# RWKV-7 time mixing on one core: transpositions, masks and head sums moved within a head pair's chain

## The chip, the cores and the metric

The program runs on 1 core of one Trainium2 chip. Its engines are TensorE (PE; PEld is its weight load), VectorE (DVE), ScalarE (ACT), GpSimd (POOL) and SyncE, whose queue (SP) issues nearly all DMAs here. The metric is the device time of one execution in microseconds (us); lower is better. Three runs of the kernel before the change gave 2665.36, 2665.69 and 2669.86 us, so the median is 2665.69 us.

## The reference, cut to what matters

The whole model is two layers: time mixing (RWKV-7) and a squared-ReLU MLP, then banded attention and an MLP, on 256 tokens of width 2048. Only time mixing is touched. It has 32 heads of 64 channels.

```python
def rwkv7_time_mix(h, mu, w_r, w_k, w_v, w_o, w0, w1, w2, a0, a1, a2, g1, g2, k_k, k_a, r_k, ln_w, ln_b):
    xr, xw, xk, xv, xa, xg = [h + xx * mu[j] for j in range(6)]
    r, k, v = xr @ w_r, xk @ w_k, xv @ w_v
    w_log = -jax.nn.softplus(-(w0 + jnp.tanh(xw @ w1) @ w2)) - 0.5
    a = jax.nn.sigmoid(a0 + (xa @ a1) @ a2)
    g = jax.nn.sigmoid(xg @ g1) @ g2
    kk = heads(k * k_k)
    kk = kk / jnp.maximum(jnp.sqrt(jnp.sum(kk * kk, axis=-1, keepdims=True)), 1e-12)
    k = k * (1 + (a - 1) * k_a)
    decay = jnp.exp(-jnp.exp(heads(w_log)))
    def step(S, inp):
        r_t, w_t, k_t, v_t, kk_t, a_t = inp
        sa = jnp.einsum('bhvk,bhk->bhv', S, -kk_t)
        S = (S * w_t[:, :, None, :] + sa[..., None] * (kk_t * a_t)[:, :, None, :]
             + v_t[..., None] * k_t[:, :, None, :])
        return S, jnp.einsum('bhvk,bhk->bhv', S, r_t)
    ...  # y from the scan, normalized per head, plus sum(r k r_k) v, times g, through w_o
```

## The kernel before, in words

The recurrence is computed in chunks of 64 tokens (C = 64, four chunks) for two heads at a time; the class `Pair` is one such pair, and there are 16 of them. Channels lie on the 128 partitions (two heads of 64), tokens on the free axis. A pair is a generator of 36 steps (each `yield` ends one): `early`, 8 steps, makes the decays (`sw`, `cum`, `e1`, `e2`), the normalized key `kk` (from the head sum `pss` of `sq`, a matmul with the block matrix `bones`), and the products `bh`, `kh`, `kr`, `rkp`, `vp`; `invert`, 12 steps, makes the inverse of a unit triangular 64x64 matrix per head and chunk; `late`, 16 steps, walks the four chunks with the state `zs`, and then normalizes `y`, with a second head sum `var`.

`invert` starts from the Gram product `gr` (tile `pg`, line 210). ACT copies its blocks out as `da` and `co` (lines 218 and 220); `u` starts as identity plus a masked `da` (line 221 on POOL, line 227 on DVE), and `als` (line 223, POOL) holds the masked blocks of four more levels. Each level l of the loop at line 237 takes two steps: first a transposition of `u` on DVE (line 239, tile `tt`), 32x32 matmuls of it with `als` into the PSUM tile `iv`, and a copy `xs` by ACT; then matmuls of `xs` with `u` and an update of `u` on DVE (line 254). In the last level `uf` is written: its diagonal blocks by POOL (line 249), its corner by DVE (line 258).

The order of the work is set by the loop over slots in `layer_a` (line 889). A pair starts every 8 slots, so up to five pairs are alive, at steps 8 apart. In each slot every living pair takes one step, pairs in `invert` first, then `late`, then `early`; the PE work of each is put behind that of the one before by `issue_after`. Behind these small matmuls PE gets a piece of dense work: four of the 32 k-tile pieces of this pair of heads' k and r projections (line 853; lines 412 and 413 are their matmuls), or, when all projections are done, of the output projection. In three slots of four, from slot 16 on, one piece of an adaLN vector is accumulated on DVE (line 454, tile `acc`, from a 512 KB load of `w_ada`, tile `raw`). Weights come in fp32 and are split into two halves: `wH` by an ACT cast (line 378), `wL` by a DVE subtraction (line 381).

```python
for _, _, pr in sorted(live, key=lambda x: x[:2]):
    with tc.issue_after(last):
        next(pr.gen)
    last = self.last_pe()
```

PE's order is so written out; each of the other engines takes its queue in order too, and the framework's planner fills that queue: what comes earlier in the program goes first when it is expected to be ready. Waits between engines, and waits for a buffer of a tile to come free, are set by the framework, which also keeps two engines from accessing one PSUM bank tile at once in an order other than the program's. PSUM tiles: `gr` and `iv` have one buffer, `ms` (all products of odd kinds, through `psm`) two, `lt` (a bank of `late`) two, `pj` (projections) two. SBUF tiles `s`, `sl`, `bh`, `kh`, `u`, `tt`, `xs` and the like rotate over the number of buffers given at the call.

Of the kernel before, what the change touches and what calls it, by code (L numbers as in the profile page):

```python
# [25 lines left out]
C = 64  # L26
# [51 lines left out]
class Pair:  # L78
# [43 lines left out]
    def early(self):  # L122
# [19 lines left out]
        pss = b.psm()[:, :T]  # L142
        self.head_sums(pss, sq)
# [8 lines left out]
        yield  # L152
        rs, ss, rr = s(), s(), s()
# [16 lines left out]
        nc.vector.tensor_tensor(out=kr[:, :, 0:C], in0=ch(kk), in1=e0, op=ALU.mult)  # L170
        nc.vector.tensor_tensor(out=self.bh, in0=self.bh, in1=kk, op=ALU.mult)
        nc.vector.tensor_tensor(out=kr[:, :, C:P], in0=ch(r), in1=e1, op=ALU.mult)
        rkp = s()
        nc.vector.scalar_tensor_tensor(out=rkp, in0=r, scalar=vec("r_k", j), in1=km, op0=ALU.mult, op1=ALU.mult)
# [17 lines left out]
    def invert(self):  # L192
# [11 lines left out]
        ts = []  # L204
        for src in (bh, kh):
            t = s()
            nc.gpsimd.tensor_tensor(out=ch(t), in0=ch(src), in1=self.pc.to_broadcast([P, 4, C]), op=ALU.mult)
# [4 lines left out]
        nc.vector.tensor_tensor(out=ch(ar), in0=pg[:, :, C:P], in1=ui[:, :, C:P], op=ALU.mult)  # L212


        da, co, u = half("da", 2), half("co", 2), half("u", 2)
        for i, K in enumerate(QS):
            n = H * (i % 2)
            nc.scalar.copy(da[K], pg[K, :, n:n + H])
# [1013 lines left out]
```

## Time and profile before

| | before |
|---|---|
| median of three runs | 2665.69 us |
| the profiled execution's own time | 2668.82 us |
| span of the profiled execution | 2667.0 us |
| PE busy | 2594.2 us, 97% |
| DVE busy | 2112.8 us, 79% |
| ACT busy | 1345.2 us, 50% |
| POOL busy | 208.7 us, 8% |
| mean granted TensorE clock | 0.992 |

The time mixing's pairs run from about 219 to 715 us of the span. A row of a group reads: line, engine, operation, output<-inputs, shapes, count, then busy time in us, mean ns of one, and the idle time of the engine just before them with what ended it. A row of a timeline reads: start in us, duration in us, engine, line, operation, operands, count, and in brackets the idle time before it and what ended that. Consecutive instructions of one kind are merged in a timeline. A row of a table by stretch reads: stretch, length, busy us and count of PE, PEld, DVE, ACT, POOL, then the granted clock as a share of full speed, the busy share of the DMA engines and GB/s. PE's ends are modelled, so a busy PE may hide short waits.

### The profile page before, as it was taken

To read this page: it belongs to the slowest core of one execution; us is meant where nothing else is said; L and a number is where in the kernel's file an instruction comes from. 1 tells how busy PE (TensorE), PEld (TensorE's weight loads), DVE (VectorE), ACT (ScalarE), POOL (GpSimd) and SP (SyncE) were. 2 spreads that over 40 slices of the span, in tenths; PEclk is the share of its full clock that TensorE was granted. 3 is DMA by queue.
4 is the path that set the end of the run, shared out by engine and by line. 5 is a ranking of instruction groups with operands and counts; after the bars stand their busy time and mean duration, and the time that the engine had idled before them with its cause. 6 is when DMAs were issued, how large, how long until landed. Compare 5 with 4: busy or idle time off the path is not lost.

```text
span 2667.0 us, 58173 instructions
## 1 busy us (share of the span) xinstructions
PE 2594.2 (97%) x23596; PEld 2229.2 (84%) x23596; DVE 2112.8 (79%) x3102; ACT 1345.2 (50%) x2435; POOL 208.7 (8%) x320
## 2 busy tenths in 40 slices
PE   7999999999999999999999999999999999999997
PEld 4787777887899888888888998877898888888886
DVE  6788888889789888888888898899887555555555
ACT  3346455555456445355365554565564463453554
POOL 0002223322110000000001100000100000000002
PEclk9999999999999999999999999999999999999998
DMA  9976556566778888889898679887766555555553
GB/s 349 312 244 211 185 179 207 180 214 199 246 236 312 309 317 327 319 324 332 318 329 293 238 242 331 318 274 256 265 218 235 190 189 184 188 189 186 186 189 119
DMA packets 207149, 662.62 MB, mean 248 GB/s; under 512 B 21408, under 2 KB 54560, under 8 KB 206880
## 3 DMA queue, kind: packets, MB, share of 16 engines
q1 hardware_dynamic: 204816, 656.36, 71.5%
q8 instruction: 185, 3.03, 0.5%
q10 hardware_dynamic: 2064, 2.54, 0.3%
q14 instruction: 84, 0.69, 0.1%
HBM read 656.72 MB, written 2.10 MB: 247 GB/s over the span
## 4 chain that ended last, share of the span: by engine, by line
PE 85%; DVE 5%; issue 4%; DMA 4%; ACT 2%; POOL 1%; DVEq 0%; SPq 0%; ACTq 0%; POOLq 0%
PE pj L412 45%; PE pj L413 23%; PE pj L402 2%; PE pj L401 2%; PE pj L403 2%; DMA raw<-w_ada 1%; DVE wL L381 1%; PE iv L111 1%; DVE acc L454 1%; PE gr L105 1%; ACT wH L378 1%; PE ms L115 1%; PE o L401 1%; PE ms L324 0%; PE ms L105 0%
## 5 line engine op out<-in xcount | busy, mean ns | idle before, releaser
L381 DVE TENSOR_TENSOR wL<-raw,wH 128x1024 fp32r<-128x1024 f32 x772 | 941.1, 1220 | 354.9 <-ACT wH L378 347.0
L378 ACT CAST wH<-raw 128x1024 fp32r<-128x1024 f32 x772 | 805.8, 1045 | 799.7 <-PE pj L412 650.0
L412 PE MATMUL pj<-aHL,wH 128*128 128x512 f32 x3328 | 1202.0, 403 | 1.9 <-DVE x L945 1.4
L413 PE MATMUL pj<-aHL,wL 128*128 128x256 f32 x3328 | 936.1, 281 | 0.4 <-DVE wL L381 0.4
L412 PEld LDWEIGHTS pj<-aHL,wH 128*128 128x128 f32 x3328 | 629.4, 189 | 154.4 <-issue 8.7
L412 PE MATMUL pj<-hHL,wH 128*128 128x512 f32 x2048 | 723.0, 398 | 0.0
L413 PEld LDWEIGHTS pj<-aHL,wL 128*128 128x128 f32 x3328 | 629.4, 189 | 3.1 <-issue 0.8
L413 PE MATMUL pj<-hHL,wL 128*128 128x256 f32 x2048 | 574.4, 281 | 0.0
L412 PEld LDWEIGHTS pj<-hHL,wH 128*128 128x128 f32 x2048 | 384.6, 188 | 94.4 <-DVE hHL L991 0.2
L413 PEld LDWEIGHTS pj<-hHL,wL 128*128 128x128 f32 x2048 | 386.8, 189 | 0.1
L454 DVE SCALAR_TENSOR_TENSOR acc<-rada,ct,acc 128x1024 f32<-128x1024 f32 x256 | 327.2, 1278 | 8.5 <-DMA rada<-w_ada 7.6
L518 POOL TENSOR_TENSOR ss<-ss,sq 128x256 f32<-128x256 f32 x56 | 52.6, 940 | 1590.8 <-ACT sq L517 1590.5
L1016 DVE SCALAR_TENSOR_TENSOR x<-pj,mod,x 128x256 f32<-128x256 f32 x256 | 123.4, 482 | 58.6 <-PE pj L413 54.9
L454 DVE SCALAR_TENSOR_TENSOR acc<-raw,ct,acc 128x1024 f32<-128x1024 f32 x104 | 136.2, 1309 | 15.3 <-DMA raw<-w_ada 14.9
L988 ACT ACTIVATE t<-t 128x256 f32<-128x256 f32 x112 | 46.8, 418 | 123.5 <-DVE t L960 123.5
L401 PE MATMUL pj<-aHL,wH 128*128 128x258 f32 x384 | 109.0, 284 | 0.0
L402 PE MATMUL pj<-aHL,wH 128*128 128x258 f32 x384 | 108.9, 284 | 0.0
L403 PE MATMUL pj<-aHL,wL 128*128 128x258 f32 x384 | 108.0, 281 | 0.0
L403 PEld LDWEIGHTS pj<-aHL,wL 128*128 128x128 f32 x384 | 73.2, 191 | 0.2
L402 PEld LDWEIGHTS pj<-aHL,wH 128*128 128x128 f32 x384 | 72.6, 189 | 0.1
L401 PEld LDWEIGHTS pj<-aHL,wH 128*128 128x128 f32 x384 | 72.2, 188 | 0.2
L990 ACT ACTIVATE t<-t 128x256 f32<-128x256 f32 x128 | 53.4, 417 | 3.4
(249 smaller groups left out, 2815.5 us busy)
## 6 DMA issues: line engine op xcount, KB each, us to landing
raw<-w_up SPq DMA_DIRECT2D x256, 512.0 KB, 4.2
raw<-w_down SPq DMA_DIRECT2D x256, 512.0 KB, 4.3
rada<-w_ada SPq DMA_DIRECT2D x209, 512.0 KB, 5.8
raw<-w_ada SPq DMA_DIRECT2D x111, 512.0 KB, 4.3
rada<-w_ada_kv SPq DMA_DIRECT2D x64, 512.0 KB, 6.1
rawa<-w_ada SPq DMA_DIRECT2D x32, 512.0 KB, 6.9
rawa<-w_ada_t SPq DMA_DIRECT2D x32, 512.0 KB, 7.5
raw<-w_k SPq DMA_DIRECT2D x32, 512.0 KB, 4.0
```

The costliest lines, as they stand in the source:

```text
L378: nc.scalar.copy(Hf, raw)
L381: eng.tensor_tensor(out=Lf, in0=raw, in1=Hf, op=ALU.subtract)
L401: nc.tensor.matmul(ps, H[:, i, :], a(kt)[:, 0, :], start=(first and kt == 0), stop=False)
L402: nc.tensor.matmul(ps, H[:, i, :], a(kt)[:, 1, :], start=False, stop=False)
L403: ins = nc.tensor.matmul(ps, L[:, i, :], a(kt)[:, 0, :], start=False, stop=(last and kt == KT - 1))
L412: nc.tensor.matmul(ps, H[:, i, :], a(kt), start=(kt == 0), stop=False)
L413: ins = nc.tensor.matmul(ps[:, 0, :], L[:, i, :], a(kt)[:, 0, :], start=False, stop=(kt == KT - 1))
L454: nc.vector.scalar_tensor_tensor(out=self.acc, in0=raw, scalar=ck, in1=self.acc, op0=ALU.mult, op1=ALU.add)
L518: (eng or nc.gpsimd).tensor_tensor(out=self.ss, in0=self.ss, in1=sq, op=ALU.add)
L988: nc.scalar.activation(t, t, AF.Relu)
L990: nc.scalar.activation(t, t, AF.Square)
L1016: nc.vector.scalar_tensor_tensor(out=x, in0=ps[:, i, :], scalar=self.mods[(layer, 5)][:, n:n + 1], in1=x, op0=ALU.mult, op1=ALU.add)
```

## The change

Nothing is computed differently but for the order of some operations and the engine that does them.

- In `invert`, the transposition of `u` is no longer the first instruction of a level but the last of the update before it: a helper `turned()` issues it directly behind the start value of `u` (in the first step) and directly behind each update.
- The identity is added to `u` by GpSimd, directly behind the mask, ahead of `als`; it was DVE's, one step later.
- `ar` (the masked right half of `pg`) moves from the first step, ahead of the copies `da` and `co`, to the second.
- The corner of `uf` is copied by ACT instead of DVE.
- The factors scaled by `pc` (`ts`, two GpSimd multiplications) move from the first step of `invert` to the seventh of `early`, two steps ahead.
- In `early`, the head sum `pss` goes from the third step to the fifth; `ss` and the three activations behind it from the fourth to the fifth; `rr`, `rs` and `kk` from the fifth to the sixth; `bh`'s second product and `kr` from the sixth to the seventh. `vp` comes earlier, from the seventh to the fifth, and `rkp` from the sixth to the fifth; `km` and `kh` stay in their steps.
- In `late`, the square of `y` is taken in the last chunk's step, the head sum `var` two steps behind it, in the free half of the pair's own bank instead of an `ms` tile, and the logarithm and the addition of `v` one step earlier.

```diff
@@ -139,8 +139,6 @@
         nc.scalar.activation(sw, sw, AF.Exp, scale=-1.0, bias=b.col(C_MHALF))
         nc.scalar.activation(a, a, AF.Exp, scale=-1.0)
         yield
-        pss = b.psm()[:, :T]
-        self.head_sums(pss, sq)
         cum = s()
         nc.vector.tensor_tensor_scan(out=cum, data0=cst("reset"), data1=sw, initial=0.0, op0=ALU.mult, op1=ALU.add)
         e0, e1 = e01[:, :, 0:C], e01[:, :, 1:C + 1]
@@ -150,35 +148,41 @@
         self.pc = pw.tile([P, 4, 1], F32, tag="pc", bufs=4, name="pc")
         nc.gpsimd.tensor_copy(self.pc, e01[:, :, C:C + 1])
         yield
+        km = s()
+        nc.gpsimd.tensor_scalar(out=km, in0=a, scalar1=-1.0, scalar2=vec("k_a", j), op0=ALU.add, op1=ALU.mult)
+        self.bh, self.kh = s("bh", 2), s("kh", 2)
+        nc.gpsimd.tensor_tensor(out=self.bh, in0=a, in1=e2, op=ALU.mult)
+        yield
+        pss = b.psm()[:, :T]
+        self.head_sums(pss, sq)
         rs, ss, rr = s(), s(), s()
         nc.vector.tensor_scalar(out=ss, in0=pss, scalar1=1e-24, scalar2=None, op0=ALU.max)
         nc.scalar.activation(rs, ss, AF.Ln)
         nc.scalar.activation(rs, rs, AF.Exp, scale=-0.5)
         nc.scalar.activation(rr, rs, AF.Square)
-        km = s()
-        nc.gpsimd.tensor_scalar(out=km, in0=a, scalar1=-1.0, scalar2=vec("k_a", j), op0=ALU.add, op1=ALU.mult)
-        self.bh, self.kh = s("bh", 2), s("kh", 2)
-        nc.gpsimd.tensor_tensor(out=self.bh, in0=a, in1=e2, op=ALU.mult)
-        yield
+        self.vp = pw.tile([P, 4, C], F32, tag="vp", bufs=4, name="vp")
+        pt = b.psm().rearrange("p (a c k) -> p a c k", a=2, c=4)
+        self.each(lambda c: pt[:, 0, c, :], lambda c: ch(v)[:, c, :], lambda c: cst("cen"))
+        nc.scalar.copy(self.vp, pt[:, 0])
+        nc.vector.scalar_tensor_tensor(out=km, in0=km, scalar=1.0, in1=k, op0=ALU.add, op1=ALU.mult)
+        rkp = s()
+        nc.vector.scalar_tensor_tensor(out=rkp, in0=r, scalar=vec("r_k", j), in1=km, op0=ALU.mult, op1=ALU.mult)
+        yield
+        kr = self.kr = self.big("kr", 4)
         nc.vector.scalar_tensor_tensor(out=rr, in0=rr, scalar=-0.5, in1=ss, op0=ALU.mult, op1=ALU.mult)
         nc.vector.scalar_tensor_tensor(out=rs, in0=rr, scalar=1.5, in1=rs, op0=ALU.add, op1=ALU.mult)
         kk = s()
         nc.vector.scalar_tensor_tensor(out=kk, in0=k, scalar=vec("k_k", j), in1=rs, op0=ALU.mult, op1=ALU.mult)
-        nc.vector.scalar_tensor_tensor(out=km, in0=km, scalar=1.0, in1=k, op0=ALU.add, op1=ALU.mult)
-        yield
-        kr = self.kr = self.big("kr", 4)
+        nc.vector.tensor_tensor(out=self.kh, in0=km, in1=e2, op=ALU.mult)
+        yield
+        nc.vector.tensor_tensor(out=self.bh, in0=self.bh, in1=kk, op=ALU.mult)
         nc.vector.tensor_tensor(out=kr[:, :, 0:C], in0=ch(kk), in1=e0, op=ALU.mult)
-        nc.vector.tensor_tensor(out=self.bh, in0=self.bh, in1=kk, op=ALU.mult)
         nc.vector.tensor_tensor(out=kr[:, :, C:P], in0=ch(r), in1=e1, op=ALU.mult)
-        rkp = s()
-        nc.vector.scalar_tensor_tensor(out=rkp, in0=r, scalar=vec("r_k", j), in1=km, op0=ALU.mult, op1=ALU.mult)
-        nc.vector.tensor_tensor(out=self.kh, in0=km, in1=e2, op=ALU.mult)
-        yield
-
-        self.vp = pw.tile([P, 4, C], F32, tag="vp", bufs=4, name="vp")
-        pt = b.psm().rearrange("p (a c k) -> p a c k", a=2, c=4)
-        self.each(lambda c: pt[:, 0, c, :], lambda c: ch(v)[:, c, :], lambda c: cst("cen"))
-        nc.scalar.copy(self.vp, pt[:, 0])
+        self.ts = []
+        for src in (self.kh, self.bh):
+            t = s()
+            nc.gpsimd.tensor_tensor(out=ch(t), in0=ch(src), in1=self.pc.to_broadcast([P, 4, C]), op=ALU.mult)
+            self.ts.insert(0, t)
         yield
         pbn = b.psm()[:, :T]
         self.head_sums(pbn, rkp)
@@ -201,33 +205,34 @@
 
 
         ui = cst("ui").unsqueeze(1).to_broadcast([P, 4, P])
-        ts = []
-        for src in (bh, kh):
-            t = s()
-            nc.gpsimd.tensor_tensor(out=ch(t), in0=ch(src), in1=self.pc.to_broadcast([P, 4, C]), op=ALU.mult)
-            ts.append(t)
         pg = pp.tile([P, 4, P], F32, tag="gr", bufs=1, name="gr")
         self.each(lambda c: pg[:, c, :], lambda c: ch(bh)[:, c, :], lambda c: kr[:, c, :])
-        ar = self.ar = s("ar", 3)
-        nc.vector.tensor_tensor(out=ch(ar), in0=pg[:, :, C:P], in1=ui[:, :, C:P], op=ALU.mult)
 
 
         da, co, u = half("da", 2), half("co", 2), half("u", 2)
+
+        def turned():
+            t = half("tt", 2)
+            nc.vector.transpose(out=t.rearrange("p c t -> p (c t)"), in_=u.rearrange("p c t -> p (c t)"))
+            return t
+
         for i, K in enumerate(QS):
             n = H * (i % 2)
             nc.scalar.copy(da[K], pg[K, :, n:n + H])
             if i % 2 == 0:
                 nc.scalar.mul(co[K], pg[K, :, H:C], -1.0)
         nc.gpsimd.tensor_tensor(out=u, in0=da, in1=every("lev0"), op=ALU.mult)
+        nc.gpsimd.tensor_tensor(out=u, in0=u, in1=every("eye_h"), op=ALU.add)
+        tn = turned()
         als = b.pw.tile([P, 4, 4, H], F32, tag="al", bufs=2, name="al")
         nc.gpsimd.tensor_tensor(out=als, in0=da.unsqueeze(1).to_broadcast([P, 4, 4, H]),
                                 in1=cst("levs").rearrange("p (l k) -> p l k", l=4).unsqueeze(2).to_broadcast([P, 4, 4, H]),
                                 op=ALU.mult)
         yield
-        nc.vector.tensor_tensor(out=u, in0=u, in1=every("eye_h"), op=ALU.add)
-
+        ar = self.ar = s("ar", 3)
+        nc.vector.tensor_tensor(out=ch(ar), in0=pg[:, :, C:P], in1=ui[:, :, C:P], op=ALU.mult)
         pt = b.psm().rearrange("p (a c k) -> p a c k", a=2, c=4)
-        for i, t in enumerate(ts):
+        for i, t in enumerate(self.ts):
             self.each(lambda c: pt[:, i, c, :], lambda c: ch(t)[:, c, :], lambda c: cst("eye"))
         bk = self.bk = b.pw.tile([P, 2, 4, C], F32, tag="bk", bufs=3, name="bk")
         nc.scalar.copy(bk, pt)
@@ -235,8 +240,7 @@
         uf = self.u = b.uf[self.j % 2]
         down, up = ((0, 1), (2, 3)), ((1, 0), (3, 2))
         for l in range(1, 6):
-            tt_, xs = half("tt", 2), half("xs", 2)
-            nc.vector.transpose(out=tt_.rearrange("p c t -> p (c t)"), in_=u.rearrange("p c t -> p (c t)"))
+            tt_, xs = tn, half("xs", 2)
             pi = self.corner(l)
             if l < 5:
                 self.tiles(pi, als[:, l - 1], tt_, [(i, i) for i in range(4)])
@@ -252,10 +256,11 @@
             if l < 5:
                 self.tiles(pi, xs, u, [(i, i) for i in range(4)])
                 nc.vector.tensor_tensor(out=u, in0=u, in1=pi, op=ALU.add)
+                tn = turned()
             else:
                 self.tiles(pi, xs, u, up)
                 for K in QS[::2]:
-                    nc.vector.tensor_copy(uf[K, :, H:C], pi[K])
+                    nc.scalar.copy(uf[K, :, H:C], pi[K])
             if l == 2:
                 pg = pp.tile([P, 4, P], F32, tag="gr", bufs=1, name="gr")
                 self.each(lambda c: pg[:, c, :], lambda c: ch(kh)[:, c, :], lambda c: kr[:, c, :])
@@ -307,22 +312,23 @@
                     nc.vector.scalar_tensor_tensor(out=zn, in0=zs, scalar=pc[:, c, :], in1=pch[:, 2, :],
                                                    op0=ALU.mult, op1=ALU.add)
                 zs = zn
+            if c == 3:
+                sq = self.square(py)
             yield
 
-        sq = self.square(py)
-        yield
-        var = b.psm()[:, :T]
+        yield
+        var = bank[:, 0, :]
         self.head_sums(var, sq)
-        yield
         rg = s("sl", 1)
         nc.scalar.activation(rg, var, AF.Ln, scale=1.0 / C, bias=b.col(C_GN))
+        yield
         nc.scalar.activation(rg, rg, AF.Exp, scale=-0.5)
         nc.vector.scalar_tensor_tensor(out=rg, in0=py, scalar=b.vec("ln_w", j), in1=rg, op0=ALU.mult, op1=ALU.mult)
+        nc.vector.scalar_tensor_tensor(out=rg, in0=v, scalar=b.vec("ln_b", j), in1=rg, op0=ALU.add, op1=ALU.add)
         yield
         pg = b.psm()[:, :T]
         for i in range(2):
             mm(pg, lg[:, i, :], self.tg[:, i, :], start=(i == 0), stop=(i == 1))
-        nc.vector.scalar_tensor_tensor(out=rg, in0=v, scalar=b.vec("ln_b", j), in1=rg, op0=ALU.add, op1=ALU.add)
         nc.vector.tensor_tensor(out=v, in0=pg, in1=rg, op=ALU.mult)
         yield
```

More of the change, by code (lines that the diff above doesn't have):

```diff
@@ L166, in early @@
         nc.vector.scalar_tensor_tensor(out=kk, in0=k, scalar=vec("k_k", j), in1=rs, op0=ALU.mult, op1=ALU.mult)
-        nc.vector.scalar_tensor_tensor(out=km, in0=km, scalar=1.0, in1=k, op0=ALU.add, op1=ALU.mult)
-        yield
-        kr = self.kr = self.big("kr", 4)
-        nc.vector.tensor_tensor(out=kr[:, :, 0:C], in0=ch(kk), in1=e0, op=ALU.mult)
-        nc.vector.tensor_tensor(out=self.bh, in0=self.bh, in1=kk, op=ALU.mult)
-        nc.vector.tensor_tensor(out=kr[:, :, C:P], in0=ch(r), in1=e1, op=ALU.mult)
-        rkp = s()
-        nc.vector.scalar_tensor_tensor(out=rkp, in0=r, scalar=vec("r_k", j), in1=km, op0=ALU.mult, op1=ALU.mult)
         nc.vector.tensor_tensor(out=self.kh, in0=km, in1=e2, op=ALU.mult)
         yield
-        self.vp = pw.tile([P, 4, C], F32, tag="vp", bufs=4, name="vp")
-        pt = b.psm().rearrange("p (a c k) -> p a c k", a=2, c=4)
-        self.each(lambda c: pt[:, 0, c, :], lambda c: ch(v)[:, c, :], lambda c: cst("cen"))
-        nc.scalar.copy(self.vp, pt[:, 0])
+        nc.vector.tensor_tensor(out=self.bh, in0=self.bh, in1=kk, op=ALU.mult)
+        nc.vector.tensor_tensor(out=kr[:, :, 0:C], in0=ch(kk), in1=e0, op=ALU.mult)
+        nc.vector.tensor_tensor(out=kr[:, :, C:P], in0=ch(r), in1=e1, op=ALU.mult)
+        self.ts = []
[3 more added lines that the diff above has]
+            self.ts.insert(0, t)
         yield
```

## The prediction

> **What bounds the kernel now.** I read the page's first part, then the table by stretch for the stage that the change touches, then PE's waits there, then the timelines around the longest of them.
>
> ```profile
> span 2667.0 us, 58173 instructions
> 216.00:300.00 84.00, 74.13 (x1180) 60.59 (x1178) 70.06 (x119) 43.37 (x109) 24.44 (x32) 0.94 0.62 200
> 300.00:630.00 330.00, 323.60 (x6786) 265.44 (x6785) 287.28 (x545) 176.69 (x500) 90.56 (x123) 1.00 0.60 192
> 630.00:720.00 90.00, 82.05 (x1575) 71.28 (x1574) 73.06 (x126) 40.30 (x109) 13.72 (x21) 0.99 0.71 236
> ```
>
> The stage of the pairs is 216 to 720. PE is busy 74.1 of the first 84 us, 323.6 of the middle 330, 82.1 of the last 90: it is the bound, and all its idle time is 9.9 + 6.4 + 8.0 = 24.3 us. The change neither adds nor removes a matmul, so the idle time, and time at a lower clock, is all that it can win. DVE is busy 83%, 87% and 81% of the three stretches: it is no bound in the middle but close to one, and its queue is what PE waits for:
>
> ```profile
> PE o L403 <- DVE wL L381: 3.2, 1, 3.2
> PE iv L111 <- DVE tt L239: 12.2, 10, 4.1
> L115 PE MATMUL ms<-s,csts 128*128 128x256 f32 x32 | 11.2, 431 | 1.6 <-DVE s L174 1.6
> L324 PE MATMUL ms<-tg,lg 128*128 128x256 f32 x64 | 17.9, 401 | 2.8 <-issue 1.4 <-DVE s L154 1.2
> ```
>
> Half of PE's idle time is ten waits for the transposition `tt` (12.2 us, the longest 4.1). By stretch they are 8.5, 2.1 and 1.8 us:
>
> ```profile
>   PE iv L111: 8.5, 5
> ...
>   PE iv L111: 2.1, 4
> ...
>   PE iv L111: 1.8, 2
> ```
>
> The two longest show their making. In the first fence `u` was done at 274.39, but its transposition ran at 277.80, behind 3.4 us of other DVE work that the program puts ahead of it; PE had waited since 274.1. In the second, the transposition stood behind an `acc` that waited for its load.
>
> ```profile
> 274.11 0.28 DVE L254 TENSOR_TENSOR u<-u,iv 128x128 f32<-128x128 f32 x1
> ...
> 277.80 0.30 DVE L239 STREAM_TRANSPOSE tt<-u 128x128 f32<-128x128 f32 x1
> ...
> 278.24 0.65 PE L111 MATMUL iv<-tt,al 32*32 32x32 f32 x32 [4.15 <-DVE tt L239]
> ```
>
> ```profile
> 237.10 1.28 DVE L454 SCALAR_TENSOR_TENSOR acc<-raw,ct,acc 128x1024 f32<-128x1024 f32 x1 [0.29 <-DMA raw<-w_ada]
> 238.30 0.30 DVE L239 STREAM_TRANSPOSE tt<-u 128x128 f32<-128x128 f32 x1
> ...
> 238.75 0.45 PE L111 MATMUL iv<-tt,al 32*32 32x32 f32 x32 [2.36 <-DVE tt L239]
> ```
>
> Behind both, the granted clock falls:
>
> ```profile
> 240.00:244.00 4.00, 4.00 (x45) 3.16 (x44) 2.77 (x6) 1.54 (x4) 1.63 (x3) 0.57 0.77 202
> 276.00:288.00 12.00, 9.76 (x168) 8.22 (x170) 7.45 (x12) 2.04 (x5) 1.87 (x2) 0.72 0.48 155
> ```
>
> The lost work is about 4.00 x (1 - 0.57) = 1.7 us and, over the 9.76 busy us of the second, about 9.76 x 0.28 = 2.7 us (taking the stretch's mean clock for its busy part): 4.4 us.
>
> **The change part by part.** *Transposition behind the update.* 80 transpositions stay 80, at 0.30 us. Directly behind `u`, the one of 274.11 would end near 274.7, and PE would start at 274.8 by the same 0.14 us from end to start (278.10 to 278.24), so about 0.7 of the 4.1 us stays; the other waits of the first stretch go wholly as far as `u` itself is in time. The gain there lies between 0 (the wait only moves, see below) and 8.5 - 0.7 + 4.4 = 12.2 us. The `tt` tiles are held a step longer, with two buffers; as both pairs in `invert` write in the same odd slot and their matmuls read in the next, I count nothing for that. What is queued behind the earlier transposition on DVE (`mk`, `zs`, `wL`) comes 0.30 us later, and an `acc` no longer stands ahead of it.
>
> Why not all 12.2: DVE is busy 70.1 of the 84 us. It sheds three or so of the 1.18 us identity additions and two pairs' corner copies (below), near 4.5 us, and so needs at least 65.5; PE without low clock needs 74.1 - 4.4 = 69.7. Both would have to run with almost no idle time for the whole gain. I take 7.5 us, somewhat over half, since the two long waits, which carry the clock with them, are cut by order alone. In the middle and the end the waits are 2.1 + 1.8 = 3.9 us: I take 2.8.
>
> *Identity on GpSimd, corner on ACT, `ar` later.*
>
> ```profile
> L227 DVE TENSOR_TENSOR u<-u,csts 128x128 f32<-128x128 f32 x16 | 18.6, 1161 | 6.3 <-POOL u L221 5.3
> L254 DVE TENSOR_TENSOR u<-u,iv 128x128 f32<-128x128 f32 x64 | 18.1, 282 | 9.0 <-PE iv L111 8.0
> L258 DVE COPY uf<-ms 32x128 f32<-32x128 f32 x32 | 9.0, 281 | 0.9 <-PE ms L111 0.6
> L221 POOL TENSOR_TENSOR u<-da,csts 128x128 f32<-128x128 f32 x16 | 10.8, 672 | 181.2 <-ACT da L218 181.2
> ```
>
> DVE loses 18.6 + 9.0 = 27.6 us; GpSimd gets 16 x 0.67 = 10.8 us (by L221, the same size) and ACT 32 x 0.25 = 8 us (by the 0.25 us copy of the same size in the next fence, at 489.55). Neither is near full (129 and 260 us of the 504 above), so none of this is on PE's path by itself. The identity addition is dear on DVE: 1161 ns against 282 for an update of the same size. What stands beside it is `als` on GpSimd (next fence: 491.72 for 1.09 us, against 491.79 for 1.18). I read this as the two shutting each other out; the transposition, of one input, does not (492.89, two in 0.49 us, beside `uf` copies).
>
> The start of each pair's inverse now reads: `gr`, six ACT copies, mask, identity, transposition. One pair in the middle:
>
> ```profile
> 486.30 1.09 PE L105 MATMUL gr<-kr,bh 64*64 64x128 f32 x16
> ...
> 489.10 0.41 DVE L212 TENSOR_TENSOR ar<-gr,csts 128x256 f32<-128x256 f32 x1
> 489.43 0.87 DVE L132 TENSOR_SCALAR s<-ms,vecs 128x256 f32<-128x256 f32 x2
> 490.21 1.27 DVE L454 SCALAR_TENSOR_TENSOR acc<-raw,ct,acc 128x1024 f32<-128x1024 f32 x1
> 491.41 0.28 DVE L254 TENSOR_TENSOR u<-u,iv 128x128 f32<-128x128 f32 x1
> 491.79 1.18 DVE L227 TENSOR_TENSOR u<-u,csts 128x128 f32<-128x128 f32 x1
> 492.89 0.49 DVE L239 STREAM_TRANSPOSE tt<-u 128x128 f32<-128x128 f32 x2
> ...
> 489.55 0.25 ACT L218 COPY da<-gr 32x128 f32<-32x128 f32 x1 [1.77 <-DVE ar L212]
> ...
> 491.03 0.73 POOL L221 TENSOR_TENSOR u<-da,csts 128x128 f32<-128x128 f32 x1 [11.73 <-ACT da L218]
> 491.72 1.09 POOL L223 TENSOR_TENSOR al<-da,csts 128x512 f32<-128x512 f32 x1
> ...
> 494.35 0.34 PE L111 MATMUL ms<-tt,co 32*32 32x32 f32 x10
> ```
>
> Before, the copies waited 1.77 us for `ar`; with `ar` behind them they can start when ACT is free. From their start to the mask is 491.03 - 489.55 = 1.5 us, then 0.73 + 0.73 + 0.30. If they start near 487.8 (`gr` ends at 487.4), the first transposition ends near 491.1. DVE, in order, may stand before it from 489.1, where it did `ar`: up to 1.7 us idle. Then come the 0.87 and 1.27 us (491.1 to 493.2), the other pair's update (to 493.5) and its transposition (to 493.8). PE took that one at 494.35. So the new wait fits, with 0.5 us to spare, and the planner may fill it with other work. I take 0.13 us for each of 16 pairs, 2 us, between 0 and 16 x 1.3 = 21.
>
> *Scaled factors.* `ts` is as many instructions, and GpSimd already ran ahead to them and waited for `bh`; `bk` needs them in the second step of `invert`, two slots after their new place. Nothing.
>
> ```profile
> POOL s L207 <- DVE bh L171: 103.2, 16, 9.0
> ```
>
> *Head sums.* The 1.6 us wait for `rkp` (L174) should go with `rkp` a step earlier and its sum where it was. With `pss` out of the slots between `var` and the gate's product, and `var` out of the `ms` tiles (eight a pair instead of nine), L324's 1.2 us waits for `ss` (L154) go too. I count 1.4 of the 2.8, as the saturated DVE of the first stretch may delay what follows. Cost: `pss` and `kk` are nearer to `gr`, which needs `bh` and `kr` one slot after they are made instead of two. A slot is 57.2 / 16 = 3.58 us (the two `gr` below lie two pairs apart); DVE ran 1.7 us behind PE in the fence above (487.4 to 489.1). I take nothing; at worst DVE's 1.27 us `acc` stands ahead of `kr` in half the pairs, 8 x 1.27 = 10 us, and at best it is nothing, since no instruction is saved.
>
> ```profile
> 391.06 1.02 PE gr L105 x16
> ...
> 448.29 1.02 PE gr L105 x16
> ```
>
> No DMA is added or passed on SP's queue; `raw` loads start earlier only as their tiles come free earlier, and the DMA engines are busy 0.60 to 0.71. The 3.2 us wait for `wL` at the end stays.
>
> Sum: -7.5 - 2.8 + 2.0 - 1.4 = -9.7 us. The profiled execution would go from 2668.8 to 2659.1; it was 3.1 us above the median, so the median goes from 2665.7 to **2656.0 us**; its own range is 2647 (12.2 + 3.9 + 2.8 us of gains and no cost) to 2660.4.
>
> **Two rules.** The Trainium skill, "SBUF — State Buffer", section "SBUF: two separate sides", says that DVE with two SBUF inputs and a GpSimd instruction that reads SBUF exclude each other for a whole instruction, whoever starts second waiting. The trace agrees (1161 against 282 ns), and it speaks against the change: the identity on GpSimd may wait out an `acc` of 1.28 us. By that rule at its worst the sum would be -9.7 + 16 x 1.28 = +10.8 us; by the row that I took, it is -9.7.
>
> The page "TensorE: Matmul & The Clock Gate", section "What's actually happening", in the Trainium skill, gives about 3.4 us of idle time before the clock halves. By that, a wait of 2.36 us would cost no clock, the clock's part would be 2.7 instead of 4.4 us, and the sum about 1 us smaller; here the clock was 0.57 behind just that wait, so the row decides.
>
> **The rivals.** *The wait moves (no change).* In the first stretch DVE stays the partner bound, and `acc` still stands in its queue when a load is late:
>
> ```profile
> DVE acc L454 <- DMA raw<-w_ada: 14.9, 13, 2.8
> ```
>
> PE then waits for `u` or `wL` where it waited for `tt`. For it: DVE 70 of 84 us. Against it: 3.4 us of the longest wait were order alone. The first stretch's 7.5 becomes 1.5: 2666 - 3.7 = 2662. The planner leaving `tt` behind other work, so that the change doesn't do what it says, ends there too.
>
> *DVE stands before the first transposition (slower).* Place: step one of each `invert`. GpSimd's copies show what waiting beside DVE does: four in 1.59 us once, and in 2.68 where they began beside DVE's identity addition (491.79 to 492.97).
>
> ```profile
> 293.17 1.59 POOL L249 COPY uf<-u 32x128 f32<-32x128 f32 x4 [0.41 <-DVE u L254]
> ...
> 492.76 2.68 POOL L249 COPY uf<-u 32x128 f32<-32x128 f32 x4
> ```
>
> Point of decision: the transposition more than 0.5 us later than 491.1, that is mask and identity at 2.0 us together instead of 1.5. At 1.3 us over it, all pairs lose 16 x 1.3 = 21 us against the 11.7 of the gains: +9.3, 2675. Against it: DVE stands idle then, so no `acc` runs beside GpSimd.
>
> **How the numbers follow.** A measurement of this kernel can tell about 0.2%, 5.3 us, from no change. Forecast 0.60, the wait moves 0.20, slower 0.20: so faster 0.60, same 0.20, slower 0.20. The range 2645 to 2673 takes in the forecast and the second case and leaves out the far end of the slower one and gains beyond 20.7 us; its low end is 2 us below the forecast's own range, for short waits that a busy PE hides.
>
> **What would show it.** Right: L239's share of PE's waits near zero, the clock near 1.00 from 236 to 288, no L227 on DVE, `als` directly behind an addition on GpSimd. Wrong: DVE waiting for GpSimd before L239's successor in 16 places, or PE idle for `u`, `wL` or `gr` in the first stretch as long as before. A loss in the middle stretch, where only 6.4 us were idle, would overturn the argument.

## The result, and the profile after

The change makes the kernel slower: 2676.03 us (median of 7 runs, 2672.48 to 2680.85) against 2667.27 us (7 runs, 2665.36 to 2669.86) for the kernel before beside it. The ratio is 1.0031, with a 95% interval of 1.0019 to 1.0043, so +8.8 us where the forecast was -9.7. The profiled execution took 2676.03 us. First its page: the span, and the busy time of PE.

```profile
span 2674.2 us, 58153 instructions
...
PE 2597.7 (97%) x23596; PEld 2227.9 (83%) x23596; DVE 2091.8 (78%) x3054; ACT 1355.2 (51%) x2467; POOL 212.9 (8%) x336
```

The table by stretch, as in the prediction (stretch, its length, busy time of PE, PEld, DVE, ACT and POOL, granted clock, DMA share, GB/s):

```profile
216.00:300.00 84.00, 76.56 (x1354) 61.83 (x1352) 68.38 (x119) 47.09 (x118) 26.26 (x36) 0.98 0.64 209
300.00:630.00 330.00, 316.99 (x6490) 256.14 (x6478) 265.22 (x493) 178.88 (x509) 87.12 (x132) 1.00 0.59 188
630.00:720.00 90.00, 86.15 (x1692) 74.24 (x1687) 72.82 (x124) 39.99 (x117) 17.84 (x24) 1.00 0.67 221
```

PE is busier than before in the first 84 us (76.6 against 74.1, at a clock of 0.98 against 0.94) and less in the middle 330 (317.0 against 323.6). So the gain came where it was forecast, and the loss is in the middle, where the prediction said that a loss would overturn it. How much, is seen best by the same work in both: the `gr` matmuls of the 4th and the 16th pair, with 12 pairs between them. The view of the tile `gr` in two short windows gives the first and last start in each, before and then after:

```profile
L105 PE MATMUL gr<-kr,bh x16: 269/269/320, 314.6 to 315.4; 64*64 64x128 f32 x16
...
L105 PE MATMUL gr<-kr,bh x16: 269/269/320, 653.6 to 654.5; 64*64 64x128 f32 x16
```

```profile
L105 PE MATMUL gr<-kr,bh x16: 269/269/320, 309.3 to 310.1; 64*64 64x128 f32 x16
...
L105 PE MATMUL gr<-kr,bh x16: 269/269/320, 660.8 to 661.6; 64*64 64x128 f32 x16
```

The 4th pair comes 5.3 us earlier than before (309.3, 314.6), the 16th 7.2 us later (660.8, 653.6): the twelve pairs take 351.5 us instead of 339.0, and lose 12.5. The span grew by the same 7.2 us, so behind the pairs nothing changes. The table by stretch, for just these twelve pairs, splits the loss, before and then after:

```profile
314.60:653.60 339.00, 330.57 (x6946) 271.74 (x6942) 296.75 (x563) 184.34 (x525) 96.83 (x132) 1.00 0.60 194
```

```profile
309.30:660.80 351.50, 336.57 (x6950) 272.74 (x6944) 284.71 (x530) 191.78 (x549) 97.62 (x144) 1.00 0.59 191
```

PE was idle 8.4 us before and 14.9 after (+6.5), and its busy time grew by 6.0 for the same work. DVE did 12.0 us less and yet held PE up. The waits of the stage of the pairs (216 to 725; microseconds in total, times, longest) name a new first for DVE:

```profile
DVE tt L216 <- POOL u L225: 22.3, 16, 1.7
DVE wL L387 <- ACT wH L384: 20.5, 16, 2.4
...
PE iv L111 <- DVE tt L216: 13.5, 16, 2.5
```

DVE stands before the first transposition of all 16 pairs, for the identity on GpSimd: the sign of being wrong that the prediction named. PE's waits for `tt` are no fewer than before (15.7 us, 13.5 at `iv` and 2.2 at `ms`, against 12.2); in the middle 330 us they grew from 2.1 to 9.1, the 7.7 and 1.4 of these rows:

```profile
PE iv L111 <- DVE tt L216: 7.7, 10, 1.4
PE lt L285 <- DVE zs L312: 2.8, 3, 1.2
PE ms L111 <- DVE tt L216: 1.4, 3, 0.6
```

The timeline of one pair's start shows why DVE stands (rows of GpSimd, DVE and PE; start, duration, and in brackets the idle time before):

```profile
490.27 0.73 POOL L224 TENSOR_TENSOR u<-da,csts 128x128 f32<-128x128 f32 x1 [7.82 <-ACT da L221]
...
490.97 2.18 POOL L228 TENSOR_TENSOR al<-da,csts 128x512 f32<-128x512 f32 x1
490.99 1.22 DVE L387 TENSOR_TENSOR wL<-raw,wH 128x1024 fp32r<-128x1024 f32 x1
...
493.12 0.41 POOL L225 TENSOR_TENSOR u<-u,csts 128x128 f32<-128x128 f32 x1
...
493.56 0.31 DVE L216 STREAM_TRANSPOSE tt<-u 128x128 f32<-128x128 f32 x1 [0.96 <-POOL u L225]
```

The program has mask, identity, `als`. GpSimd's queue has mask, `als`, identity, here and in all 16 pairs: the planner, which takes what is expected to be ready, put `als`, which needs only `da`, ahead of the identity, which needs the mask. So the identity starts at 493.12 instead of about 491.0. `als` makes it 1.10 us later (its median here); in this pair, beside DVE's `wL`, it took 2.18, its longest. Over the 16 pairs, by the same rows of each, the mask starts 2.62 us and the identity ends 4.91 us after the start of `gr`: 2.29 us for the two, beyond the 2.0 that the prediction gave its slower rival as the point of decision. (This mean, and the like below, is over the 16 pairs.)

### The profile page after: what moved, and what is told of

Same layout as the page of the kernel before. It is cut to its first block, busy times and chain, and to the rows that moved or that the text cites. A ratio compares the mean times of both kernels' runs of the same rounds, so it can differ in the third digit from the quotient of the medians.

```text
span 2674.2 us, 58153 instructions
## 1 busy us (share of the span) xinstructions
PE 2597.7 (97%) x23596; PEld 2227.9 (83%) x23596; DVE 2091.8 (78%) x3054; ACT 1355.2 (51%) x2467; POOL 212.9 (8%) x336
## 4 chain that ended last, share of the span: by engine, by line
PE 84%; DVE 6%; issue 3%; DMA 3%; POOL 2%; ACT 2%; DVEq 0%; SPq 0%; ACTq 0%; POOLq 0%
PE pj L418 44%; PE pj L419 22%; PE pj L408 2%; PE pj L407 2%; PE pj L409 2%; DVE acc L460 2%; PE iv L111 1%; DVE wL L387 1%; PE gr L105 1%; DMA rada<-w_ada 1%; PE ms L115 1%; PE o L407 1%; POOL al L228 1%; PE ms L105 0%; PE pT L1126 0%
```

## The experiments

Ratios are to the kernel before, run beside each in five rounds. "Pair 4" is the start of its `gr`, "12 pairs" the time from there to that of pair 16, and the last two columns divide it by PE's busy time, as in the two rows above; all three are from the profiled execution. A part of PE's busy time there is a lower clock: the granted clock falls to 0.50 for 3.4 us at a time, which costs 1.7 us, once within the twelve pairs of kernels 1, 7 and 10, twice in 11, three times in 9, and not in the others.

| kernel | time / before [95%] | us to before | pair 4 | 12 pairs | PE busy | PE idle |
|---|---|---|---|---|---|---|
| before | 1 | 0 | 314.6 | 339.0 | 330.6 | 8.4 |
| after | 1.0031 [1.0019, 1.0043] | +8.8 | 309.3 | 351.5 | 336.6 | 14.9 |
| 1 after, identity ahead of `als` | 0.9976 [0.9967, 0.9986] | -6.1 | 305.8 | 345.5 | 336.6 | 8.9 |
| 2 after, identity on DVE | 0.9982 [0.9974, 0.9990] | -5.4 | 304.2 | 344.4 | 336.8 | 7.6 |
| 3 transposition alone | 0.9964 [0.9951, 0.9976] | -9.1 | 303.9 | 339.4 | 330.4 | 9.0 |
| 4 head sums alone | 0.9980 [0.9972, 0.9989] | -4.9 | 303.1 | 345.3 | 335.6 | 9.7 |
| 5 head sums, `vp` ahead | 0.9980 [0.9970, 0.9989] | -5.3 | 308.3 | 341.1 | 331.5 | 9.6 |
| 6 identity alone | 1.0020 [1.0010, 1.0029] | +4.0 | 314.1 | 343.3 | 331.7 | 11.6 |
| 7 parts 3 and 5 | 0.9970 [0.9959, 0.9982] | -7.9 | 304.2 | 341.0 | 333.3 | 7.7 |
| 8 after, with 1 and `vp` ahead | 0.9978 [0.9969, 0.9987] | -5.8 | 309.3 | 341.1 | 331.7 | 9.4 |
| 9 part 3, identity behind `als` | 1.0015 [1.0006, 1.0023] | +4.1 | 307.4 | 353.1 | 335.5 | 17.6 |
| 10 part 3, identity ahead of `als` | 0.9997 [0.9988, 1.0005] | -1.3 | 304.0 | 344.1 | 331.1 | 13.0 |
| 11 part 3, `acc` behind `tt` | 0.9989 [0.9981, 0.9998] | -2.2 | 308.4 | 346.9 | 332.8 | 14.2 |
| 12 part 3, `late` of after | 0.9963 [0.9951, 0.9975] | -9.4 | 306.1 | 337.2 | 330.4 | 6.8 |

**1. The order in GpSimd's queue.** The kernel after, with an order edge that puts `als` behind the identity:

```diff
-        nc.gpsimd.tensor_tensor(out=u, in0=u, in1=every("eye_h"), op=ALU.add)
+        ins = nc.gpsimd.tensor_tensor(out=u, in0=u, in1=every("eye_h"), op=ALU.add)
...
+        with b.tc.issue_after(ins.ins):
+            nc.gpsimd.tensor_tensor(out=als, ...
```

> The changed kernel, with GpSimd made to add the identity ahead of the level masks (als); in the changed kernel its queue has them the other way round in all 16 pairs. Theory A (DVE stands before the first transposition because the identity waits out als): DVE's wait of 22.3 us for the identity falls below 8 us, PE's 15.7 us of waits for the transposition fall by 5 us or more, and the time falls from +8.8 us against the kernel before to between -4 and +2. Theory B (the head sums' new places make the loss): still +7 to +11, with DVE's wait gone. Theory C (the planner puts other DVE work between an update and its transposition, so moving it wins nothing, and the loss is from there): +4 to +9.

The time is 2662.64 us: one edge turns +8.8 us into -6.1, about 15 us, and past the -4 to +2 expected. Of the 11.7 us between the two profiled spans, 3.5 lie ahead of the 4th pair and 6.0 in the twelve pairs. There PE and DVE are busy as long as in the kernel after (336.6 and 285.0 us), and all of the 6.0 us are idle time of PE:

```profile
305.80:651.30 345.50, 336.61 (x6956) 273.10 (x6944) 285.00 (x530) 191.08 (x549) 99.37 (x144) 1.00 0.61 194
```

DVE's order changes little with the edge: 748 of the 783 instructions that it runs between 200 and 740 us in the kernel after come in the same order here. Mask start to identity end is now 1.37 us, below the point of decision, and the waits of the stage are

```profile
DVE tt L216 <- POOL u L225: 10.8, 16, 0.9
PE iv L111 <- DVE tt L216: 9.0, 11, 1.1
```

DVE still waits 10.8 us, 0.7 in a pair, not under 8 as expected. One pair shows a cause (GpSimd's rows, then DVE's):

```profile
483.08 1.26 POOL L224 TENSOR_TENSOR u<-da,csts 128x128 f32<-128x128 f32 x1 [7.82 <-ACT da L221]
484.42 1.39 POOL L225 TENSOR_TENSOR u<-u,csts 128x128 f32<-128x128 f32 x1
485.77 1.10 POOL L229 TENSOR_TENSOR al<-da,csts 128x512 f32<-128x512 f32 x1
```

```profile
482.79 1.28 DVE L461 SCALAR_TENSOR_TENSOR acc<-raw,ct,acc 128x1024 f32<-128x1024 f32 x1 [3.13 <-DMA raw<-w_ada]
...
484.32 1.22 DVE L388 TENSOR_TENSOR wL<-raw,wH 128x1024 fp32r<-128x1024 f32 x1
485.84 0.31 DVE L216 STREAM_TRANSPOSE tt<-u 128x128 f32<-128x128 f32 x1 [0.30 <-POOL u L225]
```

The mask took 1.26 us beside `acc` and the identity 1.39 beside `wL`. That is the exclusion that the prediction read from the slow identity on DVE, at work on GpSimd. It is not the rule: the view of the tile `u` (shortest, median and longest in ns) gives 416 for the identity here, and in the kernel after, where DVE stands idle while it runs, it is never longer.

```profile
L224 POOL TENSOR_TENSOR u<-da,csts x16: 418/562/1487, 234.0 to 653.9; 128x128 f32<-128x128 f32 x16
L225 POOL TENSOR_TENSOR u<-u,csts x16: 410/416/1388, 234.5 to 654.4; 128x128 f32<-128x128 f32 x16
```

```profile
L225 POOL TENSOR_TENSOR u<-u,csts x16: 406/414/421, 233.8 to 665.9; 128x128 f32<-128x128 f32 x16
...
L228 POOL TENSOR_TENSOR al<-da,csts x16: 1085/1102/2183, 232.7 to 663.8; 128x512 f32<-128x512 f32 x16
```

The second fence is of the kernel after, with `als` below the identity. What is left of the wait is in most pairs mask and identity themselves (0.56 and 0.42 us in the median).

**2. The identity back on DVE.** The kernel after, with `nc.vector.tensor_tensor` for the identity.

> The changed kernel, with the identity added by DVE in the same place (directly ahead of the transposition). Theory A: DVE no longer waits for als by way of the identity, but the addition itself takes about 1.16 us beside als as in the kernel before, and it stands a step earlier than there; 16 x 1 us of DVE as in the changed kernel, so the time stays between +2 and +8. Theory B: +7 to +11. Theory C: +4 to +9.

-5.4 us instead of the small loss expected, like kernel 1. DVE pays as much here as in the kernel after: 16 additions of 1.17 us and 4.1 us of waits for the mask, 22.9 us against 22.3 of standing, and the first transposition ends 5.3 us behind the start of `gr` in both.

```profile
L225 DVE TENSOR_TENSOR u<-u,csts 128x128 f32<-128x128 f32 x16 | 18.8, 1174 | 4.1 <-POOL u L224 4.1
```

And yet PE is idle 7.6 us instead of 14.9. Mask start to identity end is 2.06 us here, so this kernel passes the prediction's point of decision too, and it gains. So neither the length of DVE's stand alone nor the lateness of the first transposition makes the loss. What differs beside them is DVE's order, which the planner makes anew for each kernel: only 682 of those 783 instructions come in the same order, behind the addition DVE does one other operation before the first transposition in 15 of 16 pairs, and PE waits less for the transpositions of the later steps (6.5 us against 15.7). Which of these differences counts is open.

**3 and 4. Two parts alone.** Kernel 3 is the kernel before with only the transposition moved; the identity stays on DVE, in its step, and the first transposition follows it.

```diff
         nc.vector.tensor_tensor(out=u, in0=u, in1=every("eye_h"), op=ALU.add)
+        tn = turned()
...
-            tt_, xs = half("tt", 2), half("xs", 2)
-            nc.vector.transpose(out=tt_..., in_=u...)
+            tt_, xs = tn, half("xs", 2)
...
                 nc.vector.tensor_tensor(out=u, in0=u, in1=pi, op=ALU.add)
+                tn = turned()
```

> The kernel before, with only the transposition moved behind each update and behind the identity (which stays on DVE, in its step). Theory A: a gain of 4 to 9 us, as forecast for this part, PE's waits for the transposition below 5 us. Theory B: the same gain. Theory C: no gain, within 3 us of the kernel before, since 14 of 64 updates have an accumulation (1.27 us) between them and their transposition in DVE's queue.

-9.1 us, within 1.2 of the prediction's two terms for it (7.5 + 2.8 = 10.3). PE's waits for `tt` are 6.0 us, a little over the 5 expected. By stretch, and PE's waits:

```profile
216.00:300.00 84.00, 78.73 (x1446) 64.86 (x1446) 78.17 (x136) 46.11 (x118) 25.25 (x34) 1.00 0.68 218
300.00:630.00 330.00, 322.03 (x6729) 263.81 (x6727) 286.52 (x544) 180.26 (x512) 100.32 (x130) 1.00 0.61 195
```

```profile
PE iv L111 <- DVE tt L219: 6.0, 7, 1.9
```

PE is busy 78.7 of the first 84 us at full clock, against 74.1 at 0.94, and waits for `tt` are halved (12.2 to 6.0).

Kernel 4 is the kernel before with `early` and `late` of after, the scaled factors left in `invert`.

> The kernel before, with only early and late as in the changed kernel (head sums, vp, rkp, var, without the scaled factors' move). Theory A: within 3 us of the kernel before. Theory B: slower by 6 to 11 us, the middle pairs 0.5 to 0.9 us longer each. Theory C: within 3 us.

-4.9 us: outside the 3 us of two of the theories, and faster, not slower as the third had it. But the twelve pairs take 6.3 us longer than before, 0.53 us each, as that one had said, while the 4th pair comes 11.5 us earlier. All but 1.3 us of the 6.3 is busy time of PE:

```profile
303.10:648.40 345.30, 335.60 (x6958) 272.38 (x6944) 300.32 (x564) 183.81 (x525) 92.91 (x132) 1.00 0.60 191
```

**5. Where PE's busy time comes from.** In `early` of after, the `vp` matmuls (64x64) come directly behind the `pss` sum (128x128) in PE's order; their weight load then waits:

```profile
PEld ms L105 <- issue: 3.6, 11, 0.3
```

This is 0.33 us in 11 of the 12 pairs (kernel 4, from pair 4 to 16); before, that line waited once, 1.2 us. Kernel 5 is kernel 4 with the four lines of `vp` moved ahead of `pss`.

> As e4 (early and late of the changed kernel in the kernel before), with vp's 64x64 matmuls ahead of the head sum pss in the fifth step instead of behind it. Theory D (the middle pairs of e4 are 6 us longer over 12 pairs because each pair's PE work changes between 64x64 and 128x128 tiles once more, 11 waits of 0.33 us ahead of vp's loads): these 0.3 us waits are gone, the 12 middle pairs take 341 to 342 us instead of 345.3, and the time is 3 to 5 us below e4's. Theory E (DVE's waits, for zs and the transposition, make the longer middle): within 1.5 us of e4.

The twelve pairs take 341.1 us as expected, and PE's busy time is back at 331.5:

```profile
308.30:649.40 341.10, 331.49 (x6954) 272.39 (x6944) 300.94 (x564) 183.71 (x525) 93.35 (x132) 1.00 0.61 194
```

So the order of these matmuls makes 4 of the 6 us. PE's rows show it, in one pair of kernel 4 and the same pair of kernel 5 (`lt` is the last 64x64 product ahead, `pj` the projection behind):

```profile
405.84 0.28 PE L279 MATMUL lt<-vp,mk 64*64 64x64 f32 x4
406.05 0.70 PE L115 MATMUL ms<-sq,csts 128*128 128x256 f32 x2
406.68 0.68 PE L105 MATMUL ms<-csts,v 64*64 64x64 f32 x16
...
407.63 0.28 PE L413 MATMUL pj<-aHL,wL 128*128 128x256 f32 x1
```

```profile
410.98 0.28 PE L279 MATMUL lt<-vp,mk 64*64 64x64 f32 x4
411.09 0.63 PE L105 MATMUL ms<-csts,v 64*64 64x64 f32 x16
411.66 0.70 PE L115 MATMUL ms<-sq,csts 128*128 128x256 f32 x2
...
412.43 0.28 PE L413 MATMUL pj<-aHL,wL 128*128 128x256 f32 x1
```

From the start of `lt` to that of this `pj` the same matmuls take 1.79 us in kernel 4 and 1.45 in kernel 5, without a wait in either. The difference is 0.34 or 0.35 us in each of the 12 pairs, and 12 x 0.34 = 4.1 us is the difference of the two busy times. On this way the shape changes three times in kernel 4 and once in kernel 5. The Trainium skill says that a change of the tiling mode drains TensorE ("TensorEngine Tiling (Array Packing)", "Key Properties"), and gives no price; these rows agree, with 0.34 us for two changes.

The whole is not lower by it (-5.3 against -4.9, within the intervals), so the 3 to 5 us expected of the time did not come: the 4th pair comes 5.2 us later than in kernel 4. The swap changes the planner's order on the other engines too; why the first pairs lose was not found.

**6. The identity alone.** The kernel before, with the identity on GpSimd directly behind the mask and nothing else moved.

> The kernel before, with only the identity moved to GpSimd, in the place that the program gives it in the changed kernel; the transposition stays at the start of the next level, two slots later; GpSimd's queue again has the level masks ahead of the identity. Theory A (the harm is that DVE stands before a transposition that waits for the identity): DVE's waits for the identity stay below 8 us, since the transposition comes later in DVE's queue, and the time is within 4 us of the kernel before. If the identity's place in GpSimd's queue is harmful whatever follows: slower by 8 us or more.

+4.0 us, but DVE's waits are not below 8: although the program leaves the transposition in its old place, the planner puts it early, so that it ends 0.4 us behind the identity, and DVE waits.

```profile
DVE tt L239 <- POOL u L222: 15.4, 13, 1.7
```

**7 and 8. Do the parts add?** Kernel 7 is kernels 3 and 5 together, kernel 8 the kernel after with the edge of 1 and the swap of 5.

> The kernel before with e3's transpositions and e5's early and late; identity, corner, ar and scaled factors as before. Both gained in the first 84 us, where each left little idle time, so the gains don't add up there. Theory D: 2656 to 2659, at or a little below e3 (9 us below the kernel before). Theory E: 2661 to 2664, as the middle keeps e4's length.

> The changed kernel whole, with the identity ahead of the level masks (e1) and vp ahead of pss (e5). Theory D: 3 to 5 us below e1's 2662.6, so 2658 to 2660. Theory E: within 1.5 us of e1.

-7.9 and -5.8 us. Both have the twelve pairs at 341 us, as the theory of the matmul order has it, but the times are those of the other theory: neither is faster for it than 3 and 1. The parts don't add: 3 and 4 each bring the 4th pair forward by 11 us, and 7 by 10.4, not 22. Both live from the same idle time of PE in the first 84 us, 9.9 us with the clock's part on top.

**9 and 10. The order once more, without the head sums.** Kernel 9 is kernel 3 with the identity on GpSimd and the first transposition in the same step; the planner again queued mask, `als`, identity. Kernel 10 adds the edge.

> e3 (transpositions moved, 9 us below the kernel before) with the identity on GpSimd too, with the first transposition directly behind it; the rest as before. GpSimd's queue has mask, level masks, identity. Theory A: DVE waits some 20 us for the identity, and the time is 8 to 14 us above e3. If the harm in the changed kernel needs the other parts (head sums, scaled factors): within 4 us of e3.

> e9 with the queue's order forced to mask, identity, level masks, DVE's queue as in e9. Theory A: 6 us or more below e9, DVE's wait for the identity at 10 us or less; against e3 between -2 and +5, as DVE's queue has an accumulation between an update and its transposition in 25 cases instead of 14.

Kernel 9 is at 1.0015, 13.2 us above kernel 3 in the table (2673.45 against 2659.67 as they stand): this one step takes the whole gain of the transposition, and more. Its waits, and one start of a pair on DVE:

```profile
DVE tt L219 <- POOL u L228: 25.9, 16, 1.7
...
PE ms L111 <- DVE tt L219: 10.1, 10, 1.9
```

```profile
493.91 1.28 DVE L461 SCALAR_TENSOR_TENSOR acc<-raw,ct,acc 128x1024 f32<-128x1024 f32 x1
496.94 0.31 DVE L219 STREAM_TRANSPOSE tt<-u 128x128 f32<-128x128 f32 x1 [1.75 <-POOL u L228]
497.18 0.25 DVE L260 TENSOR_TENSOR u<-u,iv 128x128 f32<-128x128 f32 x1
497.35 1.27 DVE L461 SCALAR_TENSOR_TENSOR acc<-raw,ct,acc 128x1024 f32<-128x1024 f32 x1
```

DVE stands 1.75 us; the other pair's update (497.18) waits behind it, and its transposition behind an `acc` of 1.27 us more. PE waits for that second transposition: of its 13.5 us of waits for `tt`, 10.9 lie between 4 and 11 us behind a `gr`. So here the way from DVE's stand to PE is seen. In the kernel after it is longer: only 2.2 of its 15.7 us lie there, and 10.7 between 12 and 17 us behind a `gr`, mostly with an `acc` directly ahead of the update or between it and its transposition.

PE's busy time is 5.1 us above kernel 3's (335.5 against 330.4), though its work has not changed. That is the clock: behind three single waits of PE of 1.45, 1.45 and 1.58 us it is at 0.50 for 3.4 us, 1.7 us each. So of the 13.7 us by which the twelve pairs are longer than in kernel 3, 8.6 are idle time and 5.1 the clock behind it.

Kernel 10 gives back 5.3 us of the 13.2 (expected at least 6), with DVE's wait at 11.3 us, and stays 7.8 above kernel 3 in the table, where at most 5 were expected. This is the cleanest of the comparisons: 814 of the 815 instructions that DVE runs between 200 and 740 us in kernel 9 come in the same order in kernel 10. An `acc` stands between update and transposition in 25 of 64 cases in 9 and 10, in 13 in kernel 3. The order in GpSimd's queue is thus shown to be a part of the cost here, and the rest, DVE's changed order or the wait that stays, is not divided.

**11 and 12. Two tries for more.** Kernel 11 is kernel 3 with an edge that puts a slot's `acc` behind its last transposition. Kernel 12 is kernel 3 with `late` of after.

> e3 with each slot's accumulation kept behind the slot's last transposition in DVE's queue, so that one update instead of 14 has an accumulation before its transposition. Theory C (what is left of PE's waits for the transposition, 6.0 us in e3, comes from that): these waits fall to 2 us or less and the time to 1 to 4 us below e3. If the accumulation then only comes late for something else: no change against e3, with longer waits for zs or wL.

> e3 with late of the changed kernel (the square a step earlier, var in the pair's own bank) and early as before. It takes the two L324-like waits (2.6 us on PE for ss in e3) away, as eight ms tiles a pair remain: 1 to 3 us below e3. Theory E of the head sums (the harm of e4's longer middle is in early alone): the 12 middle pairs stay at 339 to 340 us.

Kernel 11 is 6.9 us slower than kernel 3 in the table (2667.16), where a gain or no change was expected: PE's waits for `tt` go down to 3.4 us (2 expected), and DVE now waits 15.8 us for the mask (4.4 in kernel 3) and 25.4 for `wH` (15.2), and PE 10.7 for `ss` (2.6). An `acc` ahead of a transposition also fills a wait. Kernel 12 is level with 3 (2659.98), where 1 to 3 us were expected; the waits for `ss` did not go (2.8 us). The best is thus the moved transposition with the rest as before, or with `late` of after.

## Why the prediction was wrong

**The step that failed** is "Identity on GpSimd": "From their start to the mask is 491.03 - 489.55 = 1.5 us, then 0.73 + 0.73 + 0.30", and from it "the new wait fits, with 0.5 us to spare", 0.13 us a pair, 2.0 in all. The copies did start earlier, 1.14 us behind `gr` instead of 2.87, and even with `als` ahead the first transposition ended earlier than before (5.3 us behind `gr` against about 6.8). But the sum took the program's order for the queue's. `als` is ready when the mask starts and the identity is not, so the planner's rule, stated above the prediction, puts `als` ahead. The order is worth about 15 us in the kernel after (1 against it), with few changes of DVE's order beside it, and 5.3 us in kernel 10 against 9, with none to speak of. The second argument, "DVE stands idle then, so no `acc` runs beside GpSimd", holds for the identity in the kernel after, but not for what stands ahead of it: DVE's queue still has `acc` or `wL` while the mask or `als` run, and then either takes about 1 us longer (mask 1.43 and `als` 2.18 at the longest, 0.41 and 1.09 at the shortest).

The slower rival had the place and the sign: DVE standing before the first transposition in all 16 pairs, and 2.29 us for mask and identity against a point of decision at 2.0. That its 2675 us lies next to the measured 2676 is in good part chance. It reckoned with GpSimd shut out by DVE, and `als` ahead in the queue was most of it; it charged each pair for the first transposition itself, while PE took that one without waiting and paid for later ones; and it had nothing for PE's busy time, nearly half of what the twelve pairs lose. Nor is its point of decision a rule: with the order mended (1.37 us) the kernel is faster than before, but so is kernel 2, at 2.06.

The Trainium skill's rule on the shared lock ("SBUF — State Buffer", "SBUF: two separate sides") had given +10.8 us at its worst. The traces agree with it as to each pair of instructions (2.18 us for `als` beside `wL`, 1.10 as the median), but its sum is near the measured +8.8 for another reason, as kernel 1 shows, in which the lock stays and the time is -6.1.

The other rival, that the wait only moves, is not what kernel 3 shows: with the transposition moved alone, PE's busy time in the first 84 us went from 74.1 to 78.7 us while DVE's went from 70.1 to 78.2, so both could run with little idle time there.

**The other steps.** *Transposition*: forecast -10.3, alone -9.1; right in size, with its clock (1.00 in the first 84 us in kernel 3), but not in one of its reasons, that "an `acc` no longer stands ahead of it": pairing updates and transpositions in order, one stands between them in 12 of 64 cases before, in 13 in kernel 3 and in 14 in the kernel after. What shrinks is the mean time from one to the other, from 1.08 to 0.90 us in kernel 3. Its 4.4 us for the clock were a little low: 0.94 over 84 us is 5.0. In the whole change the clock between 236 and 288 went from 0.90 to 0.97 and the 4th pair came 5.3 us earlier. *Head sums*: forecast -1.4, alone -4.9, but not by the two waits named. The one for `rkp` was replaced by an equal one at the same place:

```profile
PE gr L105 <- DVE kr L179: 1.6, 1, 1.6
```

This is of the kernel after; `kr` is made one slot before `gr`, which the prediction costed at nothing in the first stretch too. The cost that it did not see is on PE, which it held to be untouched: 5.0 us of busy time in the twelve pairs of kernel 4, 4.1 of which go when `vp` stands ahead of `pss` (5 against 4). In 8 against 1 it is 4.9 us, of which 1.7 are kernel 1's lower clock. *Scaled factors*: nothing was forecast, and no run has them alone. *The sum*: the terms of transposition and head sums were added, and 3, 4 and 7 show that they share one gain. Together: 5.3 us won up to the 4th pair, 6.5 lost as idle time of PE (the identity: the edge of kernel 1 takes 6.0 back) and 6.0 as its busy time (5.0 of it with the head sums alone, the last 1.0 not divided) in the next twelve, 7.2 in all, the difference of the two spans.

Open stay: why kernel 2, whose DVE pays as much and whose first transposition comes as late, loses nothing; why kernels 5 and 8 lose in the first pairs what they win later; and what holds kernel 10 above 3.

## What to carry to other kernels

Where a planner fills the queues, a step's cost follows the queue's order, not the program's: ask for each instruction that is moved to another engine what else on that engine is ready at that time, and fix the order with an edge if it matters. An operation handed from a busy engine to an idle one isn't free if the busy one waits for it in order: 18.6 us of additions on DVE, with 5.3 of waits ahead of them, became 22.3 us of standing. Try the parts of a change apart: here one edge stood between +8.8 and -6.1 us, and the simplest part alone did as well as any.

## What the runs showed of the hardware

A change of shape in PE's order costs time that shows as busy time of PE: the same matmuls took 331.5 or 335.6 us in twelve pairs (kernels 5 and 4), by whether sixteen 64x64 products stood ahead of or behind a 128x128 sum, that is 0.34 us for two changes of shape.

GpSimd and DVE hold each other up on small instructions as on large ones. On GpSimd the identity took 0.41 us while DVE stood (the kernel after) and 1.39 beside `wL` (kernel 1). On DVE it is this row of kernel 3 (shortest, median and longest in ns):

```profile
L233 DVE TENSOR_TENSOR u<-u,csts x16: 278/1172/1190, 234.6 to 647.7; 128x128 f32<-128x128 f32 x16
```

The shortest is the one addition of the 16 that did not run beside `als`; the other 15 took 0.99 us or more.

A short wait of PE can cost more than its length: in kernel 9 three waits of 1.45 to 1.58 us were each followed by 3.4 us at a clock of 0.50, 1.7 us more. Not every such wait was: behind one of 1.90 us, at 498.99 in the same kernel, the clock stayed full.
